# Output projection as seven products of halves, with weight sums made in DRAM and the convolution norm inside attention

## The chip, the cores and the metric

The kernel runs on one core of a Trainium2 chip. The metric is the device time of one execution in microseconds (us); lower is better. The core has five engines with a queue each: TensorE (PE) multiplies matrices into PSUM, VectorE (DVE), ScalarE (ACT) and GpSimd (POOL) work on elements, SyncE (SP) issues DMAs. ScalarE and GpSimd can issue DMAs too. An engine works through its queue in order.

## The reference, cut to what matters

One layer of an encoder: 1024 positions (16 grid rows of 64 columns), 1024 channels, float32.

```python
h = rms_norm(x, norm1_g)
a, gate, q, k, v = split(h @ w_in)                 # 5 x 512 columns
u = a * sigmoid(gate)                              # convolution heads
y = layer_norm(conv31_depthwise(u) + dw_bias, conv_ln_g, conv_ln_b)
conv_out = silu(y)                                 # 1024 x 512
attn_out = neighbourhood_attention(rms_norm(q), rms_norm(k), v, rpb)   # 8 heads of 64
x = x + concat([conv_out, attn_out]) @ w_out       # 1024x1024 @ 1024x1024
h = rms_norm(x, norm2_g)
x = x + (silu(h @ w_gate) * (h @ w_up)) @ w_down   # inner width 2816
```

## The kernel before, in words

Every float32 matmul is made of three fp32r ones: each operand is split into a high part `hi` (a cast, by ScalarE) and a low part `lo` (source minus `hi`, by VectorE or GpSimd; lines 103 to 108), and `mac` (lines 110 to 114) adds hi x hi, hi x lo and lo x hi into one PSUM tile of 128 x 512. So in the profile L104 is a cast, L108 a subtraction, and L112, L113 and L114 are the three matmuls, with the PSUM tile's name before them.

The order of the instructions on each engine is the order of the program, written out by hand. `woven` is a list of small jobs, one of which is run after each `mac` (`weave`), so that other work lies between the matmuls.

The stages, with the profiled times: projections of k, the gated convolution input (gl), q and v until about 241 us, in steps (`step`) of 24 matmuls, with the 31 convolution taps beside them (VectorE's L319, and GpSimd's L345, which adds products `pr` that ScalarE makes); the last sum `u` of both is VectorE's L324. The rows of v go to DRAM (`vd`, L406) and come back as windows (`vw`). Then attention, 32 steps of one pair of heads on 128 queries each: step i multiplies scores s (L615), turns the weights of step i-2 (p, L646), and multiplies them with the values of step i-3 (o, L662). VectorE adds the bias table and takes the row's extreme (L628), ScalarE takes the exponential (L630), GpSimd scales it (L637), VectorE and ScalarE copy one half of the turned weights each (L651). After four steps ScalarE and VectorE write the output as hi and lo (`at`, L669 and L674).

Then the output projection: 8 row tiles, 2 halves of the columns (pj for the first, pk for the second), 8 blocks of 128 inputs. Between the matmuls of the first half the convolution's result is turned (y, L728), normed (L735 to L756), turned back and put through silu (z, L761); its split is `cm`. A finished tile is added to x (L775). With the second half the second norm follows (L857 to L867) and the normed rows xn are turned for h2 (t, L994).

Gate and up are already seven products of halves (m1 to m7) for each of 22 blocks. Their left sides are the quarter A11, A12 (in h2), A22 of the rows and the sums S1 to S4 of quarters, formed of rows (sn, L944) and turned one by one (sq and sp, L963); their right sides are sums of quarters of the weights (ts, L893), split by GpSimd or VectorE. The down product follows, with operands that are summed and split in the same way.

The places that the prediction speaks of are attention's loop and what fills the queues ahead of it; both stand in the functions below.

Of the kernel before, what the change touches and what calls it, by code (L numbers as in the profile page):

```python
# [30 lines left out]
def layout(v):  # L31
# [4 lines left out]
    gu = np.stack([f["w_gate"], f["w_up"]]).reshape(2, KB, P, FB, P).transpose(3, 0, 2, 1, 4)  # L36
    wd = f["w_down"].reshape(FB, P, D)
# [14 lines left out]
        "wo": f["w_out"],  # L52
# [15 lines left out]
def build(ctx, tc, a):  # L68
# [22 lines left out]
    def SM(name, n=8):  # L91
        return T("sm", [P, 8], 16, name)[:, :n]

# [93 lines left out]
    wo, woq = {}, {}  # L187

    def wo_dst(d, k0):
        def dst():  # L190
            if (d, k0 // 4) not in woq:
                woq[d, k0 // 4] = H(f"wo{d}{k0}", F32R)
            q = woq[d, k0 // 4]
            o = k0 % 4 * 1024
            hl = (q[:, o:o + 1024], q[:, o + 1024:o + 2048])
            for j in range(2):
                wo[d, k0 + j] = [w[:, j * 512:(j + 1) * 512] for w in hl]
            return hl
        return dst

    for d in range(2):
        for k0 in (4, 6, 0, 2):
            want(a["wo"][k0 * P:(k0 + 2) * P, d * 512:(d + 1) * 512].rearrange("(k p) m -> p k m", p=P),
                 f"wo{d}{k0}", wo_dst(d, k0), (pool,) * 4 if d == 0 and k0 < 4 else (pool,))
# [204 lines left out]
    pend = []  # L409

    def step(post=None, n_taps=4):
        todo = pend[:]
# [251 lines left out]

    def evac_hi(s_):
        rh, cb = order[s_]
        if rh == 0:
            at[cb] = [G(f"at{cb}{w}", F32R).rearrange("p (c t q) -> p c t q", c=4, t=2) for w in range(2)]
        act.copy(at[cb][0][:, :, rh], os_[s_])  # L669

    def evac_lo(s_, cs=slice(0, 4)):
        rh, cb = order[s_]
        hi, lo = [w[:, cs, rh] for w in at[cb]]
        dve.tensor_tensor(lo, os_[s_][:, cs], hi.bitcast(F32), OP.subtract)  # L674
# [38 lines left out]
    cm, x2, xn = [], {}, {}  # L713

    def lhs(k, t):
        if k < 4:
            return [w[:, k, t * P:(t + 1) * P] for w in cm]
        return [w[:, k - 4, t // 4, :] for w in at[t % 4]]

    def proj(t, d, acc, ks):  # L720
        for k in ks:
            mac(acc, lhs(k, t), wo[d, k], k == 4, k == 3)
            weave()

# [143 lines left out]

# [379 lines left out]
```

## Time and profile before

| | |
|---|---|
| median of 3 runs | 1063.48 us (1063.12 to 1063.6) |
| the profiled execution | 1064.03 us, its span 1062.2 us |
| granted TensorE clock | 0.999 |
| DMA | 144.05 MB in 68244 packets, mean 136 GB/s |

The profile shows one execution; its span runs from the first to the last recorded instruction, and 1.8 us of its time lie outside. "PEld" is the loading of weights into TensorE, which overlaps the matmuls. A row of the view of groups names line, engine, operation, output<-input, shape and count, then the busy time in us and the mean of one in ns, then the engine's idle time before them and what ended it.

### The profile page before, as it was taken

Reading aid. Unit: us, or ns where it says so; the run is one execution under the profiler, and the core shown is the slowest. Engines: PE = TensorE matmul, PEld = TensorE weight load, DVE = VectorE, ACT = ScalarE, POOL = GpSimd, SP = SyncE. Lnnn points to the kernel's source line nnn. Section 1 sums busy time; section 2 is a strip of 40 time slices with the busy share of each in tenths; the row PEclk is TensorE's granted clock in tenths of the full one; section 3 lists DMA queues with packets and bytes.
Section 4 is the critical chain, followed back from the end, with each engine's and each line's share of the span. In section 5 each row is a group of like instructions: output and inputs, shape, how many; then the busy total and the mean of one; then the engine's idle time right before and its main releaser. Section 6 shows DMA issues by size and latency. Waiting matters only on the chain.

```text
span 1062.2 us, 13969 instructions
## 1 busy us (share of the span) xinstructions
PE 1045.4 (98%) x5068; PEld 847.3 (80%) x5068; DVE 699.8 (66%) x1072; ACT 443.7 (42%) x874; POOL 397.3 (37%) x308
## 2 busy tenths in 40 slices
PE   7999999999999999999999999999999999999997
PEld 5788888776667888788888888888888888888886
DVE  6768998966765247666565564564655567858883
ACT  6456346626776334532323223332233344433441
POOL 0126568823542301444554544545454200002310
PEclk9999999999999999999999999999999999999999
DMA  9416681245504412032322222232132597634641
GB/s 333 164 47 225 217 257 36 75 161 154 165 34 161 136 80 99 21 129 77 136 91 104 109 99 95 104 129 100 70 131 78 194 322 276 209 99 132 205 127 43
DMA packets 68244, 144.05 MB, mean 136 GB/s; under 512 B 12496, under 2 KB 21200, under 8 KB 67536
## 3 DMA queue, kind: packets, MB, share of 16 engines
q1 hardware_dynamic: 66336, 139.95, 38.3%
q10 hardware_dynamic: 1840, 3.22, 0.9%
q8 instruction: 40, 0.66, 0.3%
q14 instruction: 28, 0.23, 0.1%
HBM read 103.99 MB, written 44.76 MB: 140 GB/s over the span
## 4 chain that ended last, share of the span: by engine, by line
PE 94%; DMA 2%; DVE 1%; ACT 1%; POOL 1%; issue 0%; SPq 0%; POOLq 0%; ACTq 0%
PE B L112 6%; PE B L114 6%; PE B L113 6%; PE A L112 4%; PE D L112 4%; PE D L114 4%; PE A L114 4%; PE D L113 4%; PE A L113 4%; PE z L113 3%; PE z L112 3%; PE z L114 3%; PE gl L114 3%; PE gl L112 3%; PE gl L113 3%; PE o L662 2%
## 5 line engine op out<-in xcount | busy, mean ns | idle before, releaser
L319 DVE SCALAR_TENSOR_TENSOR cv<-u,par,cv 128x1009 f32<-128x1009 f32 (+14 forms) x85 | 108.5, 1276 | 1.9
L345 POOL TENSOR_TENSOR pa<-pa,pr 128x1022 f32<-128x1022 f32 (+10 forms) x31 | 74.2, 2392 | 35.5 <-ACT pr L344 26.5
L104 ACT CAST op<-sr 128x512 fp32r<-128x512 f32 x77 | 47.7, 619 | 52.1 <-PE B2d L114 26.3
L108 DVE TENSOR_TENSOR op<-sr,op 128x512 fp32r<-128x512 f32 x77 | 57.1, 742 | 16.1 <-ACT op L104 16.0
L1037 DVE TENSOR_TENSOR g<-B,g 128x512 f32<-128x512 f32 x22 | 15.2, 691 | 79.0 <-PE B L114 79.0
L1209 POOL TENSOR_TENSOR ou<-ou,resm 128x512 f32<-128x512 f32 x8 | 12.2, 1530 | 144.0 <-DMA resm<-xd 142.1
L1046 ACT ACTIVATE D<-D 128x512 f32<-128x512 f32 x22 | 12.8, 582 | 113.1 <-DVE D L1045 113.1
L1032 DVE TENSOR_TENSOR u<-B,g 128x512 f32<-128x512 f32 x22 | 15.2, 691 | 62.1 <-PE B L114 62.1
L104 ACT CAST op<-wd 128x512 fp32r<-128x512 f32 x66 | 40.9, 620 | 30.7 <-DVE wd L1124 18.4
L637 POOL TENSOR_SCALAR e<-e,rs 128x288 f32<-128x288 f32 (+1 forms) x64 | 34.1, 545 | 50.2 <-DVE rs L635 42.9
L108 DVE TENSOR_TENSOR op<-wd,op 128x512 fp32r<-128x512 f32 x66 | 50.4, 764 | 1.8
L893 DVE TENSOR_TENSOR ts<-gu,ts 128x512 f32<-128x512 f32 x44 | 51.0, 1159 | 0.8
L1035 ACT ACTIVATE A<-A 128x512 f32<-128x512 f32 x20 | 11.6, 582 | 76.3 <-PE A L114 76.3
L630 ACT ACTIVATE e<-e,mx 128x288 f32<-128x288 f32 (+1 forms) x64 | 36.2, 569 | 2.0 <-DVE mx L628 2.0
L628 DVE CUSTOM_DVE_ANT_0 e<-s,tab 128x288 f32<-128x288 f32 (+1 forms) x64 | 30.1, 505 | 8.1 <-PE s L615 8.0
L344 ACT ACTIVATE pr<-u,par 128x1022 f32<-128x1022 f32 (+10 forms) x31 | 34.2, 1135 | 1.2 <-ACT vs L405 1.2
L893 DVE TENSOR_TENSOR ts<-gu 128x512 f32<-128x512 f32 x22 | 34.1, 1551 | 0.0
L646 PEld LDWEIGHTS p<-ident,e 128*96 128x96 f32 (+1 forms) x192 | 20.1, 133 | 15.2 <-issue 10.5
L944 POOL TENSOR_TENSOR xn<-xn,xn 128x512 f32<-128x512 f32 x4 | 6.9, 1732 | 57.3 <-DVE sn L944 57.3
L646 PE MATMUL p<-ident,e 128*96 128x128 f32 (+1 forms) x192 | 27.6, 280 | 0.7 <-DVE pT L651 0.6
L662 PE MATMUL o<-pT,vw 96*64 96x128 f32 (+1 forms) x384 | 28.0, 281 | 0.0
L615 PE MATMUL s<-kT,qT 64*128 64x288 f32 (+1 forms) x128 | 26.7, 495 | 0.0
(1039 smaller groups left out, 3449.6 us busy)
## 6 DMA issues: line engine op xcount, KB each, us to landing
gu<-in_gu SPq DMA_DIRECT2D x44, 512.0 KB
sr<-sd SPq DMA_DIRECT2D x77, 256.0 KB
sd<-sd SPq DMA_DIRECT2D x22, 512.0 KB
wd<-in_wd SPq DMA_DIRECT2D x44, 256.0 KB
sd<-g SPq DMA_DIRECT2D x33, 256.0 KB
x<-in_x SPq DMA_DIRECT2D x16, 512.0 KB
xd<-x SPq DMA_DIRECT2D x8, 512.0 KB
resm<-xd SPq DMA_DIRECT2D x16, 256.0 KB
```

Source lines behind the costliest of these rows:

```text
L104: act.copy(hi, src)
L108: eng.tensor_tensor(*[w[..., sl] for w in (lo, src, hi.bitcast(F32))], OP.subtract)
L112: pe.matmul(acc, lh, rh, start=start, stop=False, skip_group_check=True)
L113: pe.matmul(acc, lh, rl, start=False, stop=False, skip_group_check=True)
L114: pe.matmul(acc, ll, rh, start=False, stop=stop, skip_group_check=True)
L319: dve.scalar_tensor_tensor(acc[:, o], uc[:, i], dwk[:, c, t:t + 1], acc[:, o], OP.mult, OP.add)
L344: act.activation(pr[:, o], uc[:, i], AF.Copy, scale=dwk[:, c, t:t + 1])
L345: pool.tensor_tensor(pa[:, o], pa[:, o], pr[:, o], OP.add)
L630: act.activation(e[:, hh], e[:, hh], AF.Exp, bias=mx, scale=-1.0, accum_out=rs[:, hh:hh + 1])
L646: pe.transpose(pt[:m, g * P:(g + 1) * P], es[i][:, hh, g * m:(g + 1) * m], ident)
L662: pe.matmul(os_[s_][hh * HD:(hh + 1) * HD, hp], vw[cb, rh + g][:, c:c + HD], pTs[i][:, g, hh], start=g == 0, stop=g == 2)
L893: dve.tensor_tensor(o, l, r, OP.subtract)
```

## The change

Seven things change.

1. `w_out` is laid out as four quarter blocks B11, B12, B21, B22 (rows of attention's or the convolution's channels reversed, so that A11 is attention's output of the lower half of the rows and A12 the convolution's), and a copy of the first four gate/up blocks likewise (`w4`, `g4`).
2. The sums P1 to P4 of these blocks are made in DRAM: ScalarE's queue issues 12 copies (`sum_step` with names that end in c) and GpSimd's 12 accumulating DMAs (names in a), 1 MB or half of it each, at numbered projection steps and, for the last two, in attention's steps 3 and 6.
3. The output projection is seven products n1, n7, n4, n6, n5, n2, n3, of 4 column blocks x 4 input blocks each. n7 is added into the PSUM tiles of n1, and n5 into those of n6, with a read between; `put` adds or subtracts a tile to or from x. Left sides are A11, A12, A22 and the sums Q1 to Q4, which are held as `rf` and `df`, summed by VectorE, and split by ScalarE and GpSimd.
4. In attention's loop every second step from 3 to 17 turns a tile of the convolution and takes its statistics; the square root is made on VectorE by Newton steps in steps 19 to 21, and steps 22 to 29 scale one tile each, in place.
5. The weight parts of the first two products are cast and subtracted in attention, one a step from step 17 on.
6. The normed rows are turned once (`turn`, 64 transposes); A11 and A12 go to h2, and S1 to S4 are summed and split on turned rows.
7. The first four gate/up blocks take their sums from DRAM, their order is m1, m2 of blocks 0 to 3 first, all their splits go to GpSimd, and signs are such that sums are subtracted.

```diff
+    order = [m + h * FB // 2 for m in range(FB // 2) for h in range(2)]
+    gs = gu[order[:4]].reshape(4, 2, P, 2, 512)
+    wq = f["w_out"].reshape(2, 2, 2, P, 2, 512)[::-1].transpose(0, 4, 1, 3, 2, 5)
+    pairs = [(k, d) for k in range(2) for d in range(2)]
+    w4, g4 = [np.stack(w) for w in ([wq[k, d] for k, d in pairs], [gs[:, d, :, k] for k, d in pairs])]
...
+    def sum_step(w, n, i=None):
+        m, op = {"P1": ("B12", "B11"), "P3": ("B12", "B22"), "P2": ("P1", "B22"), "P4": ("P2", "B21")}[n[:2]]
+        rs = slice(0, P) if i is None else slice(64 * i, 64 * i + 64)
+        if n[2] == "c":
+            nc.scalar.dma_start(pw[w, n[:2]][rs], block(w, m)[rs])
+        else:
+            pool.dma_start(pw[w, n[:2]][rs], block(w, op)[rs], accum_op=OP.add, max_dma_last_dim=2048)
...
+    at_step = {
+        5: [("g4", "P1c")], 6: [("g4", "P3c")], 7: halves("P1c"), 8: halves("P3c"), 9: [("g4", "P1a")],
+        11: [("g4", "P3a")], 14: halves("P1a"), 15: halves("P3a"), 24: [("g4", "P2c")], 25: [("w4", "P2c", 0)],
+        26: [("w4", "P2c", 1)], 31: [("w4", "P2a", 0)], 32: [("g4", "P2a")], 33: [("w4", "P2a", 1)],
+        34: [("g4", "P4c")], 35: [("w4", "P4c", 0)], 36: [("w4", "P4c", 1)], 37: [("g4", "P4a")],
+    }
...
+    for n in ("B11", "P3", "P4", "P2", "P1", "B21", "B22"):
+        for j in range(2):
+            want(block("w4", n)[64 * j:64 * j + 64].rearrange("r (h e) -> (r h) e", h=2), f"{n}{j}", wq_dst(n, j))
...
+        n_steps[0] += 1
+        for args in at_step.get(n_steps[0], ()):
+            sum_step(*args)
...
+            for j in range(2):
+                act.copy(rowf[j][:, :, cb], os_[s_][:, 2 * j:2 * j + 2])
+        else:
+            a11[cb] = [w.rearrange("p (c q) -> p c q", c=4) for w in lr(G(f"a11{cb}", F32R))]
+            act.copy(a11[cb][0], os_[s_])
...
+        for j in js:
+            cs = slice(2 * j, 2 * j + 2)
+            hi, lo = [w[:, cs] for w in a11[cb]]
+            dve.tensor_tensor(lo, os_[s_][:, cs], hi.bitcast(F32), OP.subtract)
+            dve.tensor_tensor(diff[j][:, :, cb], os_[s_][:, cs], rowf[j][:, :, cb], OP.subtract)
...
+    LHS = {"n7": "Q3", "n4": "A22", "n6": "Q2", "n5": "Q1", "n2": "A12", "n3": "Q4"}
+    RHS = {"n1": "B11", "n7": "P3", "n4": "P4", "n6": "P2", "n5": "P1", "n2": "B21", "n3": "B22"}
+    CB = (0, 3, 1, 2)
+
+    def proj(p, cb, acc, cs=range(4), start=True):
+        w = wq[RHS[p]]
+        for c in cs:
+            mac(acc, lhs(p, c, cb), [w[:, o + c * 512:o + c * 512 + 512] for o in (0, 2048)],
+                start and c == 0, c == 3)
             weave()
...
+    def q_split(n, f, j, eng):
+        if j == 0:
+            qop[n] = H(n, F32R)
+        split(*[qop[n][:, o + j * 1024:o + j * 1024 + 1024] for o in (0, 2048)],
+              f[j].rearrange("p c b q -> p (c b q)"), (eng,))
...
+    def conv_norm(t):
+        y = conv_T(t)
+        st6 = SM(f"bs{t}", 6)
         dve.bn_stats(st6, y)
...
+        dve.bn_aggr(mvs[:, t], st6)
...
+            xh.extend(lr(G(f"xh{t}")))
+        act.copy(xh[t], y)
...
+        for i in range(3):
+            if i == 2:
+                yield
+            dve.tensor_tensor(q, g, g, OP.mult)
+            dve.scalar_tensor_tensor(q, q, 0.25 ** i, w, OP.mult, OP.mult)
+            dve.scalar_tensor_tensor(g, q, -3.0, g, OP.add, OP.mult)
...
+    def conv_scale(t, eng):
+        eng.tensor_scalar(xh[t], xh[t], mvs[:, t, 0:1], rc[:, t:t + 1], op0=OP.subtract, op1=OP.mult)
...
+    def conv_diff(h, c, y4):
+        tiles = lambda w: w.rearrange("p (b i j) -> p i b j", b=4, j=16)
+        d, r = [tiles(w[c // 2][:, c % 2].rearrange("p b q -> p (b q)")) for w in (diff, rowf)]
+        dve.tensor_tensor(d, y4, d, OP.subtract if h else OP.add)
+        if h == 0:
...
+    def put(t, d, acc, op=OP.add, eng=dve):
+        w = x2[t][:, d * 512:(d + 1) * 512]
+        eng.tensor_tensor(w, w, acc, op)
...
+    def read(p, cb):
+        acc = pb[cb]
+        if p == "n1":
+            put(4 + cb, 0, acc)
+            put(4 + cb, 1, acc, OP.subtract)
+        elif p == "n7":
+            put(cb, 1, acc, OP.subtract)
+            put(cb, 0, acc)
+        elif p in ("n4", "n6"):
+            put(cb, 0, acc, OP.add if p == "n4" else OP.subtract)
+        elif p == "n5":
+            put(cb, 1, acc)
+            put(4 + cb, 1, acc)
+            norm2(cb)
+        elif p == "n2":
+            put(4 + cb, 0, acc)
+        else:
+            put(4 + cb, 1, acc)
+            norm2(4 + cb)
+
+    while pos[0] < pos[1] + 3:
+        issue()
...
-        if i in (6, 12):
-            load_window(i // 6)
-        if i in (14, 22):
+        if i in (6, 18):
+            load_window(1 + i // 18)
+        if i in (17, 21, 25, 29):
             take_parts(jobs)
...
+        if i % 2 and i < 19:
+            conv_norm(i // 2 - 1)
+        if i == 19:
+            root = rsqrt(rc, mvs[:, :, 1], "rc")
+        if 19 <= i < 22:
+            next(root)
+        if 22 <= i < 30:
+            conv_scale(i - 22, dve)
+        if i == 33:
+            act.activation(warm, eps, AF.Silu)
+            conv_silu(0, 0)
...
+    SRC = {"m6": "P2", "m5": "P1", "m7": "P3", "m3": "B22", "m4": "P4"}
+    firsts = [(i, None) for i in range(4)] + [(p, pr) for pr in range(2) for p in SRC]
+    queue = firsts + [(i, j) for i in range(4, FB) for j in range(2)]
...
-    products = [(i, p) for p in ("m1", "m2", "m6", "m5", "m7", "m4", "m3") for i in range(2)]
-    products += [(i, p) for i in range(2, FB) for p in ORDER]
+    products = [(i, p) for k in (0, 2) for p in ("m1", "m2") for i in (k, k + 1)]
+    products += [(i, p) for k in (0, 2) for p in SRC for i in (k, k + 1)]
+    products += [(i, p) for i in range(4, FB) for p in ORDER]
...
+    def turn(t, j):
+        if not h2:
+            h2.extend(H(f"h2{w}", F32R).rearrange("p (k s) -> p k s", s=512) for w in range(2))
+        pt = (tp, mm)[j](f"t2{t}{j}")
+        for i in range(4):
+            kb = 4 * j + i
+            pe.transpose(pt[:, i * P:(i + 1) * P], xn[t][:, kb * P:(kb + 1) * P], ident)
+        if j == 0:
+            xT[t] = G(f"xT{t}")
+        w = lr(xT[t])[j]
+        if t < 4:
+            hi, lo = [q[:, 4 * j:4 * j + 4, t * P:(t + 1) * P] for q in h2]
+            p3 = pt.rearrange("p (k s) -> p k s", s=P)
+            act.copy(hi, p3)
+            act.copy(w, pt)
+            rest.append(lambda: dve.tensor_tensor(lo, p3, hi.bitcast(F32), OP.subtract))
         else:
...
-    def t2_one(kb):
-        pt = tp(f"t20{kb}")
-        for i in range(4):
-            pe.transpose(pt[:, i * P:(i + 1) * P], xn[i][:, kb * P:(kb + 1) * P], ident)
-        split(h2[0][:, kb, :512], h2[1][:, kb, :512], pt, (dve,))
...
+    for cb in CB:
+        load_x2(4 + cb)
+    weaves(12, s0=lambda: (weigh(31), evac_hi(7), evac_lo(7)), s1=QS("Q3", diff, 0, pool), s2=lambda: tails.pop()(), s3=lambda: read("n1", 0),
+           s4=QS("Q3", diff, 1, pool), s6=C(0, 1), s10=take)
+    group("n1", CB[1:])
+    for cb in CB:
+        load_x2(cb)
+    weaves(16, s1=C(0, 2), s5=take, s9=C(0, 3), s13=QS("Q2", diff, 0, pool))
+    group("n7")
+    weaves(16, s0=C(1, 0), s2=QS("Q2", diff, 1, pool), s4=take, s6=C(1, 1), s9=take, s12=QS("Q1", rowf, 0, pool))
+    group("n4")
+    weaves(16, s0=C(1, 2), s2=take, s5=C(1, 3), s7=QS("Q1", rowf, 1, pool), s10=take, s13=QS("Q4", diff, 0, pool))
+    group("n6")
+    weaves(16, s1=take, s3=QS("Q4", diff, 1, pool), s6=take, s9=N(0), s13=N(3))
+    group("n5")
+    while pos[0] < len(chunks):
+        issue()
...
+    plan = {
+        0: dict(s0=U(7, 0), s1=[U(7, 1), N(5)], s2=SP("S2", 0), s3=SS(3, 1, 2)),
+        1: dict(s0=U(5, 0), s1=[U(5, 1), N(6)], s2=SP("S2", 3), s3=SS(1, 1, 2)),
+        2: dict(s0=U(6, 0), s1=[U(6, 1), lambda: act.activation(warm, eps, AF.Silu)], s2=SP("S2", 1), s3=SS(2, 1, 2)),
+        3: dict(s0=SP("S2", 2), s2=SP("S1", 0), s3=SP("S1", 3)),
...
-            dve.tensor_tensor(l, acc, l, OP.add)
+            dve.tensor_tensor(l, acc, l, OP.subtract)
```

Counted over the program, TensorE goes from 4116 to 4068 matmuls of 512 columns and from 344 to 296 transposes of 128 columns; the others stay.

ScalarE's queue at the end of the projections, before (pr is a product for GpSimd's convolution taps, vs a tile of v):

```order
L344 ACTIVATE pr_1918<-u_1310,par 128x1013
L405 ACTIVATE vs_1952<-z_1886,r_104 128x512
L406 DMA vd<-vs_1952 128x512
L344 ACTIVATE pr_1959<-u_1310,par 128x1012
L405 ACTIVATE vs_1991<-z_1927,r_104 128x512
L406 DMA vd<-vs_1991 128x512
L405 ACTIVATE vs_2023<-z_1966,r_104 128x512
```

and now:

```order
L371 ACTIVATE pr_1908<-u_1330,par 128x1014
L432 ACTIVATE vs_1937<-z_1868,r_112 128x512
L433 DMA vd<-vs_1937 128x512
L371 ACTIVATE pr_1944<-u_1330,par 128x1013
L208 DMA g4P_72<-g4P_70 16x16384
L432 ACTIVATE vs_1979<-z_1911,r_112 128x512
L433 DMA vd<-vs_1979 128x512
L371 ACTIVATE pr_1986<-u_1330,par 128x1012
L208 DMA w4P_68<-w4P_66 16x8192
L432 ACTIVATE vs_2019<-z_1953,r_112 128x512
L433 DMA vd<-vs_2019 128x512
L208 DMA w4P_68<-w4P_66 16x8192
```

Three copies (L208, 2 MB in all) now stand among the last products pr, the stores of v and what follows them, the first exponentials.

GpSimd's queue at the same place, before (pa is the sum of taps, e the attention weights):

```order
L345 TENSOR_TENSOR pa_1620<-pa_1620,pr_1838 128x1016
L345 TENSOR_TENSOR pa_1620<-pa_1620,pr_1841 128x1015
L345 TENSOR_TENSOR pa_1620<-pa_1620,pr_1883 128x1014
L345 TENSOR_TENSOR pa_1620<-pa_1620,pr_1918 128x1013
L345 TENSOR_TENSOR pa_1620<-pa_1620,pr_1959 128x1012
L637 TENSOR_SCALAR e_2066<-e_2066,rs_2067 128x288 x2
L637 TENSOR_SCALAR e_2109<-e_2109,rs_2110 128x288 x2
```

and now:

```order
L210 DMA w4P_66<-in_w 256x512
L372 TENSOR_TENSOR pa_1643<-pa_1643,pr_1862 128x1016
L372 TENSOR_TENSOR pa_1643<-pa_1643,pr_1865 128x1015
L210 DMA g4P_70<-in_g 512x512
L372 TENSOR_TENSOR pa_1643<-pa_1643,pr_1908 128x1014
L210 DMA w4P_66<-in_w 256x512
L372 TENSOR_TENSOR pa_1643<-pa_1643,pr_1944 128x1013
L372 TENSOR_TENSOR pa_1643<-pa_1643,pr_1986 128x1012
L210 DMA g4P_72<-in_g 512x512
L668 TENSOR_SCALAR e_2096<-e_2096,rs_2097 128x288 x2
L668 TENSOR_SCALAR e_2139<-e_2139,rs_2140 128x288 x2
L210 DMA w4P_68<-in_w 256x512
```

Five accumulating DMAs (L210) stand among the last sums of taps and the first scalings of e; the one ahead of L668 adds into what ScalarE's first copy writes.

VectorE's queue in one of attention's later steps, before:

```order
L628 ISA e_3007,mx_3009<-s_2991,tab_2356 128x384
L628 ISA mx_3009 128x1
L628 ISA e_3007,mx_3012<-s_2993,tab_2356 128x384
L628 ISA mx_3012 128x1
L651 COPY pT_3005<-p_2998 128x3x128
L674 TENSOR_TENSOR at_2824<-o_2851,at_2823 128x2x128
L635 RECIPROCAL rs_3008<-rs_3008 128x2
```

and now, where a scaling of the convolution (xh) and two residues fall together:

```order
L659 ISA e_3155,mx_3157<-s_3139,tab_2418 128x384
L659 ISA mx_3157 128x1
L659 ISA e_3155,mx_3160<-s_3141,tab_2418 128x384
L659 ISA mx_3160 128x1
L682 COPY pT_3153<-p_3146 128x3x128
L825 TENSOR_SCALAR xh_2678<-xh_2678,par 128x512
L718 TENSOR_TENSOR a_3098<-o_2986,a_3098 128x256
L719 TENSOR_TENSOR df_2536<-o_2986,rf_2342 128x2x128
L666 RECIPROCAL rs_3156<-rs_3156 128x2
```

The scaling and a second residue are added between the copy of the turned weights and the reciprocal.

391 lines of the change are left out of this document (187 added, 204 removed).

## The prediction

> **What bounds the kernel now.** I read the page first: the busy time of each engine, the granted clock and the chain of work that ended last.
>
> ```profile
> span 1062.2 us, 13969 instructions
> PE 1045.4 (98%) x5068; PEld 847.3 (80%) x5068; DVE 699.8 (66%) x1072; ACT 443.7 (42%) x874; POOL 397.3 (37%) x308
> PEclk9999999999999999999999999999999999999999
> PE 94%; DMA 2%; DVE 1%; ACT 1%; POOL 1%; issue 0%; SPq 0%; POOLq 0%; ACTq 0%
> ```
>
> TensorE is busy for 98% of the span, carries 94% of the chain, and its clock is full in every slice. The view of its waits then tells how much of the rest is a wait on another engine (line, engine waited for, total us, times, longest):
>
> ```profile
> PE z L112 <- ACT wk0h L104: 6.9, 1, 6.9
> PE z L113 <- POOL w23l L108: 0.7, 1, 0.7
> PE p L646 <- DVE pT L651: 0.6, 1, 0.6
> PE t L994 <- DVE xn L867: 0.6, 1, 0.6
> ```
>
> Apart from the first weights there is no wait of 1 us. So in the part that the change touches, work taken from TensorE is worth its own duration, as long as the other engines keep up. The prices come from two views: the table of windows (length, then busy us and instruction count of PE, PEld, DVE, ACT and POOL, then clock, DMA share and GB/s), and pieces of the chain (start, us, what).
>
> ```profile
> 100.00:150.00 50.00, 50.00 (x223) 41.40 (x222) 45.80 (x44) 19.43 (x21) 32.83 (x17) 1.00 0.79 245
> 260.00:311.00 51.00, 51.00 (x467) 33.12 (x468) 38.83 (x139) 39.62 (x120) 28.93 (x52) 1.00 0.35 112
> 290.00:311.00 21.00, 21.00 (x190) 13.51 (x188) 16.00 (x56) 16.55 (x50) 12.73 (x23) 1.00 0.20 64
> 600.00:800.00 200.00, 200.00 (x884) 165.62 (x883) 109.49 (x133) 59.26 (x108) 100.64 (x75) 1.00 0.29 106
> ```
>
> ```profile
> 296.86 0.85 PE s L615 x4
> 297.71 0.81 PE p L646 x6
> 298.51 0.81 PE o L662 x12
> 320.76 0.44 PE y L728 x4
> 395.95 0.44 PE t L994 x4
> 425.54 0.44 PE sq L963 x4
> 428.49 0.89 PE sp L963 x8
> ```
>
> From 600 to 800 us TensorE does nothing but 512-column matmuls: 200 / 884 = 0.2262 us each. Four 128-column transposes cost it 0.44 us, eight 0.89. One attention step with a 384-column window is 0.85 + 0.81 + 0.81 = 2.47 us by its pieces; from one s piece to the next I use 2.44.
>
> **The change, term by term.** The sum is made against the profiled execution, 1064.03 us, which is 0.55 us above the median of the runs.
>
> *Products of halves.* Before, the output projection is 8 row tiles x 2 column halves x 8 k blocks x 3 matmuls = 384; after it, 7 products x 4 column blocks x 4 k blocks x 3 = 336. That is 48 x 0.2262 = 10.9 us less on the chain.
>
> *Rows turned once.* Before, the second norm's rows are turned in 8 groups for h2 and 20 for S1 to S4 and A22, four transposes each; after it, in 16. That is 12 x 0.44 = 5.3 us less. The 32 conv transposes (y) only move into attention, and the 32 of z stay beside the projection: nothing.
>
> Together 16.1 us less, to 1047.9, if nobody makes TensorE wait. The following terms ask that.
>
> *Conv norm in attention.* VectorE's rows by shape, and one of ScalarE's (count, then busy us and mean ns):
>
> ```profile
> L735 DVE BATCH_NORM_STATS2 bs<-y 128x6 f32<-128x512 f32 x8 | 5.6, 695 | 2.4 <-PE y L728 2.4
> L755 DVE SCALAR_TENSOR_TENSOR bb<-bm,br 128x1 f32<-128x1 f32 x6 | 1.8, 304 | 0.4 <-DVE br L747 0.2
> L752 DVE TENSOR_SCALAR xh<-y,bm,br 128x512 f32<-128x512 f32 x2 | 1.6, 810 | 0.1
> L736 DVE BATCH_NORM_AGGREGATE bm<-bs 128x2 f32<-128x6 f32 x8 | 1.5, 182 | 0.3
> L674 DVE TENSOR_TENSOR at<-o,at 128x256 fp32r<-128x256 f32 x12 | 4.9, 412 | 0.0
> L775 DVE TENSOR_TENSOR x<-pk,x 128x512 f32<-128x512 f32 x8 | 5.5, 687 | 6.0 <-PE pk L114 6.0
> L104 ACT CAST wo<-wo04r 128x256 fp32r<-128x256 f32 x4 | 1.6, 391 | 0.0
> ```
>
> In steps 3 to 17 every second step gets statistics (0.695 + 0.182 us on VectorE) but also 0.44 us of transposes. VectorE needs 38.83 / 51 of the time there, 1.86 us of 2.44; 2.74 of 2.88 in such a step is still under. The tight place is steps 19 to 29: 11 x 2.44 = 26.8 us of TensorE, in which VectorE now has 11 x 1.86 = 20.4. Added are 14 instructions of the square root by Newton steps on 128x8, with no row of their own, between 0.18 (the aggregate's) and 0.30 us (the 128x1 row): 2.5 to 4.2. Two more of the 0.41 us residues fall there: 0.8. Eight scalings of 512 columns run from SBUF in place; the nearest rows are 0.41 (half the columns, two inputs) and 0.81 (the same operation out of PSUM): 3.3 to 6.5. So VectorE needs 27.0 to 31.9 us of 26.8: a loss of 0 to 5. I take 2, under the middle, because a row's exponentials are read two steps later, which lets about a step's slack absorb a peak. ScalarE has 16.55 of 21 there, 1.92 a step, and gains one 128x256 cast a step (0.39): 2.3 of 2.44, no loss by itself.
>
> The Trainium skill, page "VectorE: DVE Perf Modes", section "Why PSUM operands drop a tier", says that fp32 tensor_scalar reads at double rate from SBUF and not from PSUM; by its tier table I estimate 0.42 us. With that, the lower end of the loss would be the likely one and the sum 2 us less. No row of before shows that form. The page "GPSIMD Engine Reference", section "Specifications", speaks against it: such two-port instructions contend with GpSimd, which is at work here in each step.
>
> *Hand-over from the first product to the second.* n7 accumulates in n1's four banks, each of which VectorE must first add into two tiles. On VectorE's queue stand 4 residues of attention's last output, then conv's difference, which waits for GpSimd's half of Q3, and behind it the adds.
>
> ```profile
> L104 ACT CAST w23h<-w23r x1: 1032/1032/1032, 191.6 to 191.6; 128x1024 fp32r<-128x1024 f32 x1
> L108 POOL TENSOR_TENSOR w23l<-w23r,w23h x1: 2399/2399/2399, 195.6 to 195.6; 128x1024 fp32r<-128x1024 f32 x1
> ```
>
> A half is 128x1024: cast 1.03, subtraction 2.40. Counted from the second block of n1: 0.7 for three matmuls, 0.8 for the last o, 0.6 for ScalarE's copy of it (between its 0.39 and 1.03), two residues 0.8, cast and subtraction 3.4, then two conv sums and two adds at 0.69: 9.1. TensorE asks for the bank after 36 matmuls (8.1), that o (0.8) and one turning (0.4): 9.3. The margin is about zero; each us of lag from attention goes against it. Between nothing and 2 us lost, I take 0.7. The later products leave VectorE 1 to 2 adds per 2.7 us and need nothing that tight.
>
> *Sums of weight blocks in DRAM.* ScalarE's queue issues 12 copies, GpSimd's 12 accumulating DMAs, some 8 MB each; before has no accumulating one. Their issues, and SP's 12 more DMA issues, lie beside TensorE's matmuls. What matters is who stands behind. Timeline rows of GpSimd, VectorE, ScalarE and TensorE (start, us), and the longest load on the chain:
>
> ```profile
> 208.97 7.29 POOL L345 TENSOR_TENSOR pa<-pa,pr 128x1014 f32<-128x1014 f32 x3 [0.52 <-ACT pr L344]
> 231.38 0.99 POOL L637 TENSOR_SCALAR e<-e,rs 128x288 f32<-128x288 f32 x2 [15.11 <-DVE rs L635]
> 228.15 1.22 DVE L324 TENSOR_TENSOR u<-cv,pa 128x1024 f32<-128x1024 f32 x1
> 209.43 0.33 ACTq L406 DMA_DIRECT2D vd<-vs  x1
> 212.44 1.14 ACT L344 ACTIVATE pr<-u,par 128x1012 f32<-128x1012 f32 x1 [0.40 <-ACT vs L405]
> 240.98 0.86 PE L646 MATMUL p<-ident,e 128*96 128x128 f32 x6
> 13.06 7.97 DMA ag10r<-in_ag
> ```
>
> GpSimd issues g4's P2 sum at about 209; ScalarE's copy to P4 waits for it, with the last conv product and the stores of v behind; GpSimd's sum into P4 waits for the copy, with the first scaling of e behind (231.4, read by TensorE at 241.0). GpSimd has 22 us, and 8.6 more before TensorE notices: 31. The sum moves about 3.1 MB and the copy 2.1. At the 245 GB/s of the busiest window that is 13 + 9 = 22 us; two 512 KB loads like ag10r, one for each, doubled for 1 MB, give 32. So 0 to 1 us, and I take 0. ScalarE's wait ends at 222 at the 13 us, and the conv product of 212.4 starts 10 us late; its sum, which GpSimd ended at 216.3, is read by VectorE at 228.15, 12 us later. That cover is thin: without it u and with it the first scores are late, 1:1.
>
> *The rest.* Minus signs cost nothing. For the first four gate/up blocks the DRAM sums replace VectorE's, and GpSimd makes one split of some 1.4 us per product of 12 matmuls (2.7), which is free. VectorE and ScalarE now split turned rows: in the first eight products VectorE has 12 residues, 10 sums and one 1024-column scaling, 24 x 0.69 = 17 us, or, beside GpSimd at the price of
>
> ```profile
> L893 DVE TENSOR_TENSOR ts<-gu,ts 128x512 f32<-128x512 f32 x44 | 51.0, 1159 | 0.8
> L108 POOL TENSOR_TENSOR t2m<-gu,t2m 128x512 fp32r<-128x512 f32 x3 | 4.4, 1451 | 5.3 <-ACT t2m L104 5.3
> ```
>
> 22 x 1.16 + 1.4 = 27 us, against 24.3 of TensorE (eight products, six turnings). Products of S2 begin only with the ninth, those of S1 with the eleventh, so I take nothing.
>
> The sum: 1064.0 - 10.9 - 5.3 + 2.0 + 0.7 = 1050.5; less 0.55 is 1050.0 for a median.
>
> **Rivals.**
>
> *VectorE becomes the bound in attention.* For: the 31.9 of 26.8 at the upper prices, and a peak at steps 27 and 28, where two residues and a scaling fall together. Against: its idle time now, 24% there. With 5 us there and 2 at the hand-over: 1047.9 + 7 - 0.5 = 1054.4; up to 1059 if 5 us more go in steps 3 to 18, where it needs 2.74 of 2.88 us in every second step.
>
> *The DMA chain stops GpSimd before the first e scaling: slower than before.* One place, one price: TensorE pays 1:1 for each us by which sum plus copy exceed 31. The forecast gain is gone, and 2.1 us more, at 31 + 13.5 + 2.1 = 47 us. At 64 GB/s, the lowest rate of a window above, the sum alone takes 49 us, with 9 for the copy 58: 27 late, so 1050 + 27 = 1077. Against: that window is slow because little was asked for. The Trainium skill, page "DMA: Bandwidth & Descriptors", section "Issuing engines are not separate DMA queues", says that transfers of all issuers run on the same 16 engines, and "Anatomy of one DMA" gives a fit of 2 us plus the bytes at 436 GB/s, which I estimate as 4.4 us each; by it this rival is out, but no run shows an accumulating transfer.
>
> *Gain not delivered.* If weight loads or tables come late because 16 MB more are moved beside a window with a DMA share of 0.79, TensorE waits in the projections; 10 us late gives 1060, and near 1062 it is no change. Against: outside that window the share is 0.2 to 0.4.
>
> **How the numbers follow.** The measurement can tell about 0.2%, 2.1 us, from no change. The likeliest case, both savings with 0 to 5 us lost, has 0.62 (1046.5 to 1052.5); VectorE as the bound 0.20 (1052.5 to 1059); late loads 0.08, half of it within 0.2%; the DMA chain 0.10, nearly all slower. Faster is 0.62 + 0.20 + 0.04 = 0.86, same 0.04, slower 0.10. For 8 in 10 the range runs from 1046 (no loss at all gives 1047.4, and the short waits p and t may go) to 1059.
>
> **What would show it.** Right: 48 fewer 512-column matmuls and 48 fewer transposes, PE busy near 1029 us, and a PE wait list without a new entry above 1 us except on VectorE between steps 19 and 29 and at the start of n7. Wrong: a wait of p on GpSimd's e near 231 to 245, an idle stretch of TensorE behind ScalarE's copies, or VectorE at 100% in 290 to 320 with p or s waiting in each step.

## The result: slower by 1.2%

The changed kernel takes 1075.66 us (median of 4 runs, 1072.17 to 1079.1) against 1063.53 before: a ratio of 1.0115, interval 1.0082 to 1.0148. That is 12 us slower where 13.5 us faster was forecast. The profiled execution took 1075.09 us, span 1073.3. Lines of its page:

```profile
span 1073.3 us, 13909 instructions
PE 1037.3 (97%) x4972; PEld 838.5 (78%) x4972; DVE 723.2 (67%) x1097; ACT 463.1 (43%) x911; POOL 456.5 (43%) x342
...
PEclk9999978999999999999999999999999999999999
...
q0 software_dynamic: 4288, 8.39, 4.7%
...
PE 71%; DMA 10%; POOL 5%; issue 5%; SPq 3%; DVE 3%; ACT 3%; ACTq 0%; POOLq 0%; DVEq 0%
...
g4P<-in_g POOLq DMA_DIRECT2D x4, 1024.0 KB, 11.6
w4P<-in_w POOLq DMA_DIRECT2D x8, 512.0 KB, 9.1
```

The saving is there: 96 matmuls and transposes fewer. But TensorE's part of the chain of work that ended last fell from 94% to 71%, that of transfers rose from 2% to 10%, and the granted clock dips in the sixth and seventh slice (about 134 to 188 us). Queue q0, new, is GpSimd's 12 accumulating DMAs; the last two rows are their issues with the median time from issue to landing. TensorE's waits:

```profile
PE z L122 <- ACT wk0h L114: 7.4, 1, 7.4
PE z L122 <- ACT w02h L114: 4.1, 1, 4.1
PE o L693 <- DMA vw<-vd: 3.3, 1, 3.3
PE z L123 <- POOL pa L367: 2.2, 1, 2.2
PE z L123 <- POOL w01l L118: 1.9, 1, 1.9
PE z L123 <- POOL w02l L118: 1.6, 1, 1.6
PE p L677 <- DVE rcq L818: 1.5, 2, 1.2
PE t L1054 <- DVE xn L950: 1.2, 1, 1.2
PE B L124 <- POOL t0m L118: 1.1, 1, 1.1
PE B L122 <- DVE u L1172: 0.8, 1, 0.8
```

Of these the list of before has the first and, with 0.6, the one on xn. Four belong to the splitting of q's weights (w01r to w03r are the rows as loaded, h and l their high and low parts; the row that names pa is the wait for w03l), long before any code that the output projection touches. To see how much is lost where, take the row of the attention outputs in the view by tile: count, then shortest, median and longest ns, then first and last start. Before, and after:

```profile
L662 PE MATMUL o<-pT,vw x384: 272/273/324, 243.9 to 319.6; 96*64 96x128 f32 x96, 128*64 128x128 f32 x96
```

```profile
L693 PE MATMUL o<-pT,vw x384: 272/273/476, 261.6 to 347.7; 96*64 96x128 f32 x96, 128*64 128x128 f32 x96
```

| us | to the first o | first to last o | last o to the end | span |
|---|---|---|---|---|
| before | 243.9 | 75.7 | 742.6 | 1062.2 |
| after | 261.6 | 86.1 | 725.6 | 1073.3 |
| difference | +17.7 | +10.4 | -17.0 | +11.1 |

**The first stretch.** The table of windows from 60 to 100 and from 130 to 170 us (columns as in the prediction), before and after:

```profile
60.00:100.00 40.00, 40.00 (x186) 33.09 (x185) 30.14 (x35) 27.75 (x86) 22.09 (x10) 1.00 0.41 130
...
130.00:170.00 40.00, 40.00 (x182) 33.14 (x181) 35.40 (x38) 19.29 (x25) 28.73 (x14) 1.00 0.64 186
```

```profile
60.00:100.00 40.00, 40.00 (x185) 33.09 (x185) 30.42 (x36) 27.78 (x86) 24.20 (x12) 1.00 0.84 207
...
130.00:170.00 40.00, 29.54 (x103) 22.14 (x102) 27.95 (x24) 12.30 (x13) 23.08 (x11) 0.75 0.80 258
```

From 60 to 100 us nothing is lost, and the DMA engines are busy at 0.84 instead of 0.41. The bill comes later: from 130 to 170 TensorE issues 103 matmuls instead of 182, at a mean clock of 0.75. TensorE's timeline there, after:

```profile
146.98 0.39 PE L124 MATMUL z<-w00h,hT 128*128 128x512 f32 x1
147.99 0.50 PE L122 MATMUL z<-w01h,hT 128*128 128x512 f32 x1 [0.62 <-ACT w01h L114]
150.42 0.80 PE L123 MATMUL z<-w01l,hT 128*128 128x512 f32 x1 [1.93 <-POOL w01l L118]
...
157.02 0.79 PE L122 MATMUL z<-w02h,hT 128*128 128x512 f32 x1 [4.10 <-ACT w02h L114]
...
164.55 0.79 PE L123 MATMUL z<-w03l,hT 128*128 128x512 f32 x1 [2.17 <-POOL pa L367]
...
169.84 0.63 PE L123 MATMUL z<-w01l,hT 128*128 128x512 f32 x1
170.27 0.49 PE L124 MATMUL z<-w01h,hT 128*128 128x512 f32 x1
170.59 0.40 PE L122 MATMUL z<-w01h,hT 128*128 128x512 f32 x1
```

From 147.21, where the last undisturbed matmul's 0.226 us end, to 170.59 there are 23.4 us with 27 matmuls, which at full clock are 6.1. Five waits are 10.5 us (0.62, 1.93, 4.10, 1.65, 2.17). Of the other 6.8, up to 5.4 go to the clock: matmuls start 0.43 us apart (169.84 to 170.27) instead of 0.23, at a granted clock of 0.50 from 150 to 170 us, until 6 us after the last wait. The rest lies at the ends and restarts around the waits. So 10.5 us of waiting cost 17.3.

ScalarE, which makes the high parts, waits for the transfer itself. Its cast of w01, before and after:

```profile
129.54 1.05 ACT L104 CAST w01h<-w01r 128x1024 fp32r<-128x1024 f32 x1 [1.06 <-DMA w01r<-in_qkv]
```

```profile
146.89 1.05 ACT L114 CAST w01h<-w01r 128x1024 fp32r<-128x1024 f32 x1 [14.47 <-DMA w01r<-in_qkv]
```

GpSimd isn't held up ahead of this: its half of ag13 starts at 112.39 before and at 112.38 after. Before, it had the low parts of w01, w02 and w03 ready 11, 7 and 4 us ahead of their first matmuls. That was all the slack there was.

Why q's weights are late is told by SP's queue, which loads them in order between the bias tables. The same issues, before and after (start, us):

```profile
125.19 0.53 SPq L141 DMA_DIRECT2D w01r<-in_qkv  x1
...
133.45 0.53 SPq L141 DMA_DIRECT2D w02r<-in_qkv  x1
```

```profile
143.00 0.53 SPq L151 DMA_DIRECT2D w01r<-in_qkv  x1
...
151.25 0.53 SPq L151 DMA_DIRECT2D w02r<-in_qkv  x1
```

Both start the tables at the same time (66.2 and 66.5); w01 and w02 are issued 17.8 us later in the changed kernel, and the lag grows on the way: 8.1 us at ag13 (89.19 and 97.29), 16.2 at ag03 (101.39 and 117.59). SP's own longest waits for transfers between 63 and 160 us (us in total, times, longest), before and after:

```profile
SPq L481 <- DMA t<-neg: 0.6, 1, 0.6
```

```profile
SPq L507 <- DMA t<-in_rpb: 6.0, 3, 3.4
SPq L512 <- DMA tf<-neg: 3.6, 4, 2.4
SPq L512 <- DMA t<-in_rpb: 2.2, 1, 2.2
```

Before, SP waits 0.6 us for transfers in that stretch: it issues without a gap. After, it waits for its small table transfers to land, 11.8 us in these three rows; shorter waits and issues that take longer make up the rest of the 17.8. In the trace SP's issues use eight semaphores in turn, and each waits for the transfer that used its semaphore before. So when transfers land later, the whole queue slows.

**The second stretch.** ScalarE's timeline at the end of the projections:

```profile
235.48 0.69 ACT L432 ACTIVATE vs<-z,r 128x512 f32<-128x512 f32 x1 [7.28 <-DMA g4P<-in_g]
...
244.66 0.69 ACT L432 ACTIVATE vs<-z,r 128x512 f32<-128x512 f32 x1 [6.36 <-DMA g4P<-g4P]
```

The first wait is that of the copy to g4's P4 for the sum into g4's P2. The second, at a copy to w4's P4, ends with the landing of the copy to g4's P4, which used the same semaphore. The scaling of v and its stores stand behind both: TensorE then waits 3.3 us for v's reload (vw).

### The profile page after: what moved, and what is told of

It is laid out like the page before. It is cut to its first block, busy times and chain, and to the rows that moved or that the text cites. A ratio compares the mean times of both kernels' runs of the same rounds, so it can differ in the third digit from the quotient of the medians.

```text
span 1073.3 us, 13909 instructions
## 1 busy us (share of the span) xinstructions
PE 1037.3 (97%) x4972; PEld 838.5 (78%) x4972; DVE 723.2 (67%) x1097; ACT 463.1 (43%) x911; POOL 456.5 (43%) x342
## 3 DMA queue, kind: packets, MB, share of 16 engines
q0 software_dynamic: 4288, 8.39, 4.7%
q10 hardware_dynamic: 2224, 11.61, 3.0%
## 4 chain that ended last, share of the span: by engine, by line
PE 71%; DMA 10%; POOL 5%; issue 5%; SPq 3%; DVE 3%; ACT 3%; ACTq 0%; POOLq 0%; DVEq 0%
PE B L122 5%; PE B L123 5%; PE B L124 5%; PE D L122 4%; PE D L123 4%; PE D L124 4%; PE A L122 3%; PE A L123 3%; PE A L124 3%; PE z L123 2%; PE z L122 2%; PE z L124 2%; DMA t<-in_rpb 2%; DMA vd<-vs 2%; PE o L693 2%
## 5 line engine op out<-in xcount | busy, mean ns | idle before, releaser
L114 ACT CAST op<-wd 128x512 fp32r<-128x512 f32 x66 | 40.8, 619 | 29.8 <-DVE wd L1267 17.3
L668 POOL TENSOR_SCALAR e<-e,rs 128x288 f32<-128x288 f32 (+1 forms) x64 | 34.6, 553 | 39.5 <-DVE rs L666 23.4
L976 DVE TENSOR_TENSOR ts<-ts,gu 128x512 f32<-128x512 f32 x36 | 43.3, 1202 | 0.6
L1178 ACT ACTIVATE A<-A 128x512 f32<-128x512 f32 x18 | 10.5, 582 | 68.6 <-PE A L124 68.6
L863 DVE TENSOR_TENSOR x<-x,n 128x512 f32<-128x512 f32 x40 | 26.1, 680 | 18.0 <-PE n L124 11.0
L976 DVE TENSOR_TENSOR ts<-gu 128x512 f32<-128x512 f32 x18 | 30.0, 1665 | 0.0
L693 PEld LDWEIGHTS o<-pT,vw 96*64 96x64 f32 (+1 forms) x384 | 20.7, 138 | 9.4 <-issue 5.8
## 6 DMA issues: line engine op xcount, KB each, us to landing
g4P<-in_g POOLq DMA_DIRECT2D x4, 1024.0 KB, 11.6
```

The source lines that it names most:

```text
L114: act.copy(hi, src)
L668: pool.tensor_scalar(es[i][:, hh], es[i][:, hh], rs[:, hh:hh + 1], 1.0, op0=OP.mult, op1=OP.mult)
L693: pe.matmul(os_[s_][hh * HD:(hh + 1) * HD, hp], vw[cb, rh + g][:, c:c + HD], pTs[i][:, g, hh], start=g == 0, stop=g == 2)
L976: dve.tensor_tensor(lr(tsum[i, 1])[n - 3] if o is None else o, l, r, OP.add)
```

## The experiments

All are medians against runs of the kernel before on the same chip (1063.3 to 1063.6).

### Is it the sums, and are they enough alone?

e1_no_sums, the change with all 24 DMAs taken out and plain blocks in the sums' places:

```diff
-        return a[w][BLK[n]] if n in BLK else pw[w, n]
+        return a[w][BLK.get(n, int(n[1]) - 1)]
     def sum_step(w, n, i=None):
+        return
```

> The changed kernel without its 12 copies and 12 accumulating DMAs: the products read unsummed weight blocks, so the output isn't the reference's; everything else is as in the change. Theory A (the sums' traffic slows SP's queue of small bias-table transfers, so that q's weights land late and TensorE waits and loses its clock) and theory B (ScalarE and GpSimd stand still behind waits for the sums) both say 1049 to 1055 us, the forecast's 1050 with its small stalls. Theory C (the loss is in attention, the hand-over and the turned rows) says 1068 or more.

Measured: 1056.65 us (1052.19 to 1058.87), ratio 0.9931 (0.9906 to 0.9957). Without the DMAs the change is faster than before, but by less than the sum said, and just outside the 1049 to 1055 expected. A wait of 4.9 us at the hand-over between the first products is in its profile, where VectorE's adds wait for the loads of x's rows.

e2_before_sums, the kernel before with the same 24 DMAs and nobody who reads them:

```diff
+        for args in at_step.get(n_steps[0], ()):
+            sum_step(*args)
```

> The kernel before, with the same 12 copies and 12 accumulating DMAs at the same steps, whose results nobody reads. Theory A: 17 to 27 us over before, 1080 to 1090, with a wait of z for w01 to w03 of 10 us or more. Theory B: 5 to 12 us over before, 1069 to 1075, and no wait for w01 to w03. Theory C: within 3 us of before.

Measured: 1085.48 us (1084.82 to 1087.81), ratio 1.0211 (1.0196 to 1.0227): +22 us, with the waits of the changed kernel (w02h 3.9, vw 3.5, pa 2.2, w01l 1.9). The sums cost 22 us in the kernel before too, which doesn't use them. In the changed kernel leaving out all 24 DMAs gave 19 us (1075.7 to 1056.7).

### Which part of them?

e4_copies_only leaves out GpSimd's accumulating DMAs, e3_small_copies cuts the copies into 2 KB rows:

```diff
-            pool.dma_start(pw[w, n[:2]][rs], block(w, op)[rs], accum_op=OP.add, max_dma_last_dim=2048)
+            pass
```

```diff
-            nc.scalar.dma_start(pw[w, n[:2]][rs], block(w, m)[rs])
+            nc.scalar.dma_start(pw[w, n[:2]][rs], block(w, m)[rs], max_dma_last_dim=2048)
```

> The changed kernel with the 12 copies and without the 12 accumulating DMAs, so the output isn't the reference's. If the copies (16 rows of 64 KB) make SP's queue late: 1066 to 1074, with the waits for w01 to w03 still there. If the accumulating DMAs do: 1050 to 1058, without those waits. If bytes alone count, half of the delay of SP's queue goes: 1058 to 1066.

> The changed kernel with its copies written as rows of 2 KB in place of 64 KB, the same bytes. If large pieces ahead of the small table transfers are what delays them: 1052 to 1065 and shorter waits for w01 to w03. If the bytes are: 1072 to 1080, unchanged.

Measured: e4 1052.63 us (1051.23 to 1054.46), ratio 0.9904 (0.9887 to 0.9920); e3 1075.76 (1073.75 to 1080.65), ratio 1.0123 (1.0096 to 1.0149), which is the changed kernel's time. The copies cost nothing that shows where they lie, and neither does the size of their pieces. But the first six are issued at 53 to 60 us, ahead of the tables (67.7), so e4 alone doesn't tell whether adding or place makes the difference. In e4's profile all waits on w01 to w03 are gone and attention begins as before:

```profile
L693 PE MATMUL o<-pT,vw x384: 272/273/324, 243.7 to 324.7; 96*64 96x128 f32 x96, 128*64 128x128 f32 x96
```

e6_plain_pool answers that: it keeps GpSimd's 12 DMAs at their places and takes only the accumulation out:

```diff
-            pool.dma_start(pw[w, n[:2]][rs], block(w, op)[rs], accum_op=OP.add, max_dma_last_dim=2048)
+            pool.dma_start(pw[w, n[:2]][rs], block(w, op)[rs], max_dma_last_dim=2048)
```

> The changed kernel with GpSimd's 12 accumulating DMAs as plain copies of the same blocks, rows, places and waits, so the sums are missing and the output isn't the reference's. If it is the adding that occupies the DMA engines: 1051 to 1057, as with the copies of ScalarE's queue alone, and no wait for w01 to w03. If it is GpSimd's way of issuing, whatever is moved: 1070 to 1078, as in the change. If it is traffic in the stage of the tables, of which a plain copy makes about half: 1057 to 1066.

Measured: 1062.27 us (1058.14 to 1065.86, 10 runs), ratio 0.9985 (0.9972 to 0.9998). From its page, and the row of o:

```profile
q0 software_dynamic: 2240, 8.39, 2.2%
...
g4P<-in_g POOLq DMA_DIRECT2D x4, 1024.0 KB, 7.4
w4P<-in_w POOLq DMA_DIRECT2D x8, 512.0 KB, 6.7
```

```profile
L693 PE MATMUL o<-pT,vw x384: 272/273/325, 251.8 to 332.7; 96*64 96x128 f32 x96, 128*64 128x128 f32 x96
```

Plain transfers of the same bytes take 2.2% of the 16 engines' span, 23 us, and accumulating ones 4.7%, 50 us; half of the bytes of each are issued beside the tables (69 to 104 us). SP issues w01 at 125.53 in e4, 134.33 here and 143.00 in the changed kernel: 9 and 17.5 us late, nearly in proportion to that time. Attention begins 8 and 18 us late. With 9 us of lag TensorE waits for w02 and w03 (0.7, 1.9 and 3.4 us) and not for w01, as the slack of 11, 7 and 4 us says. So traffic of GpSimd's queue slows the small transfers on SP's queue, even without adding, and with accumulation the lag is twice as long. That engine time is what they share is the likeliest reading, but not shown by itself: the packets double as well (2240 and 4288), and packet times can overlap, as DMA shares above 1 in short windows show (1.05 from 90 to 100 us). The number of packets alone can't be it on ScalarE's queue, where e3 had 6128 in place of 2224 for 3.2% in place of 3.0%.

### Does another queue for q's weights help?

e11_w0_on_act issues w00 to w03 on ScalarE's queue:

```diff
-            nc.sync.dma_start(d, src)
+            (nc.scalar if name[:2] == "w0" else nc.sync).dma_start(d, src)
```

> The changed kernel, sums as they were, with q's four weight loads (w00 to w03) issued by ScalarE's queue in place of SP's. Theory: the sums only delay SP's queue, and TensorE waits because these loads stand in that queue behind some 80 table transfers. Then TensorE's wait in 145 to 170 us goes, the tables stay late: 1056 to 1066. If the loads themselves are slowed by the traffic: 1070 to 1078.

Measured: 1069.12 us (1067.27 to 1070.98), ratio 1.0046 (1.0032 to 1.0061): 6.5 us back of the 23 by which the change lies above e4, and between the two ranges expected. The waits that named w01 to w03 are gone, but the gate's last weights (ag03, issued at 118.32) still stand behind the tables, and TensorE waits 1.8 us for their half and 3.4 for VectorE's u; vw's 3.8 stays.

### Can the sums lie elsewhere?

e7_late_sums moves them all behind the tables, from the last projection steps into attention and the output projection, and loads P3 one step later:

```diff
-        5: [("g4", "P1c")], 6: [("g4", "P3c")], 7: halves("P1c"), 8: halves("P3c"), 9: [("g4", "P1a")],
+    at_step = {34: [("w4", "P1c")], 35: [("w4", "P3c")]}
+    in_attn = {
+        2: [("w4", "P1a")], 3: [("w4", "P3a")], 7: [("w4", "P2c")], 11: [("w4", "P2a")], 15: [("w4", "P4c")],
...
```

> The changed kernel with all sums moved behind the bias tables: w_out's from the last projection steps into attention's step 19, gate/up's from attention's step 20 into the product n5; the load of P3 goes one step later. Same results. If the sums cost only where they delay SP's queue of table transfers and the first windows of v: 1049 to 1055, faster than before. If they cost wherever they run: 1066 or more.

Measured: 1073.53 us (1073.11 to 1074.1), ratio 1.0092 (1.0075 to 1.0109): a miss for 1049 to 1055. Attention begins on time (first o at 243.6) but takes 96.5 us instead of e4's 81.0. TensorE's waits:

```profile
PE p L679 <- DVE pT L684: 9.2, 3, 7.8
...
PE p L679 <- POOL e L670: 3.2, 7, 0.9
```

e8_fitted_sums puts w4's P1 and P3 into the first steps, whole, ahead of the tables, the rest where the DMA share before was low, with g4's last three in attention steps 9, 12 and 16. e9_fitted_x_early is e8 with half of x's rows loaded earlier, to take away the wait for x that e1 showed:

```diff
+        1: [("w4", "P1c")], 2: [("w4", "P3c")], 7: [("w4", "P1a"), ("w4", "P3a")],
+        24: [("g4", "P1c")], 25: [("g4", "P3c")], 26: [("w4", "P2c")], 27: [("g4", "P1a")], 28: [("g4", "P3a")],
+        29: [("w4", "P2a")], 32: [("w4", "P4c")], 34: [("w4", "P4a")], 36: [("g4", "P2c")],
+    in_attn = {9: [("g4", "P2a")], 12: [("g4", "P4c")], 16: [("g4", "P4a")]}
```

> The changed kernel with the sums moved to the stretches in which the DMA engines have room and no short transfer is waited for: w_out's P1 and P3 ahead of the bias tables, its P2 and P4 and gate/up's P1 and P3 behind them (160 to 220 us), gate/up's P2 and P4 in attention's steps 9 to 16. Same results. If what counts is which transfers the sums lie beside: 1050 to 1058. If accumulating costs wherever it runs, as the late version suggests: 1066 or more.

> The one before, and x's rows for n7 are loaded ahead of the weight P21 in SP's queue. Theory: the load of x's rows, which now waits behind a weight buffer that GpSimd frees, is what VectorE's adds and so n7 wait for, 0 to 5 us from run to run. Then 1 to 5 us below the one before and a smaller spread. If the adds are late by VectorE's own work, as the forecast had it: no difference.

Measured: e8 1066.24 us (1060.68 to 1071.97, 12 runs), ratio 1.0023 (1.0001 to 1.0044); e9 1064.36 (1061.7 to 1068.81, 12 runs), ratio 1.0011 (0.9999 to 1.0024). Both miss what was expected of them: e8 lies at the edge of its range for "costs wherever it runs", and e9 gains 1.9 us on it, within the spread. Both lose nothing before attention (first o at 243.7 in e8) and then 7 to 8 us at one place. ScalarE's timeline in e9:

```profile
273.14 0.48 ACTq L208 DMA_DIRECT2D g4P<-g4P  x1
273.72 0.47 ACT L682 COPY pT<-p 96x384 f32<-96x384 f32 x1 [7.57 <-DMA g4P<-in_g]
```

The copy to P4 stands three steps (7.3 us) behind the sum into P2, which takes 16.3 us to land; ScalarE waits for it with its share of pT behind, and TensorE waits 7.0 us for pT. In e7 ScalarE stands at a copy too, for 8.71 us, but there the wait ends with a load of v's windows (vw) on SP's queue, which used the same semaphore. Either way the queue's order gives a copy's wait to the pT behind it. This place doesn't explain all of e8: its profile is that of its fastest run, 1060.7, and others took up to 1072.

Against e9, e12_spaced and e14_apart move only those three: to steps 7, 15 and 23, and to step 18 of attention and the products n4 and n5 of the output projection. The edit of e14:

```diff
-    in_attn = {9: [("g4", "P2a")], 12: [("g4", "P4c")], 16: [("g4", "P4a")]}
+    in_attn = {18: [("g4", "P2a")]}
-    weaves(16, s0=C(1, 0), s2=QS("Q2", diff, 1, pool), s4=take, s6=C(1, 1), s9=take, s12=QS("Q1", rowf, 0, pool))
+    weaves(16, s0=C(1, 0), s2=QS("Q2", diff, 1, pool), s3=X("g4", "P4c"), s4=take, s6=C(1, 1), s9=take, s12=QS("Q1", rowf, 0, pool))
-    weaves(16, s1=take, s3=QS("Q4", diff, 1, pool), s6=take, s9=N(0), s13=N(3))
+    weaves(16, s1=take, s3=QS("Q4", diff, 1, pool), s5=X("g4", "P4a"), s6=take, s9=N(0), s13=N(3))
```

> The fitted version with x's rows early, and gate/up's last three transfers moved apart in attention: P2's sum at step 7, P4's copy at 15, P4's sum at 23 (before 9, 12, 16). Theory: the fitted version lost its time where ScalarE's queue waited 7.6 us for a sum that took 16.3 us to land and had been given 3 steps, 7.3 us; 8 steps are 19.5 us. Then the wait of p for pT of 7 us goes: 1050 to 1056, faster than before. If traffic in attention costs by itself: 1060 to 1066, as the fitted one.

> The spaced version with gate/up's last transfers away from the loads of v's windows and the last bias table: P2's sum at attention's step 18, P4's copy in the product n4, P4's sum in n5. Theory: the spaced version still lost about 6 us where a table of 1.5 MB landed 19 us after its issue beside P2's sum; then 1052 to 1057 and no wait of p of more than 1.5 us. If a sum costs the same wherever it lies: 1058 to 1064.

Measured: e12 1058.93 us (1056.09 to 1065.26, 12 runs), ratio 0.9969 (0.9951 to 0.9988); the 7 us are gone, but it misses the 1050 to 1056 expected. Its profile, of a run of 1064.6 us, has two waits of 3.6 us. One is for x's rows. The other, put down to rcq, stands behind VectorE, which waits 3.2 us for a bias table. That table took 19.0 us to land, but it was also issued 5.5 us later than in e14 (271.95 and 266.50), at the end of the sum into P2 (252.4 to 272.6) and not beside it. So in attention, too, a sum can make SP's loads late; which load it slowed isn't followed here. e14: 1053.54 us (1052.52 to 1056.27, 6 runs), ratio 0.9909 (0.9893 to 0.9924). The kernel computes all that the change computes and beats both kernels, before by 0.9% and the change by 22 us. Its page, TensorE's waits and the row of o:

```profile
PE 1028.2 (98%) x4972; PEld 833.9 (79%) x4972; DVE 718.9 (68%) x1097; ACT 463.4 (44%) x911; POOL 450.6 (43%) x338
...
g4P<-in_g POOLq DMA_DIRECT2D x4, 1024.0 KB, 14.3
```

```profile
PE z L122 <- ACT wk0h L114: 6.2, 1, 6.2
PE gl L124 <- POOL ag10l L118: 1.4, 1, 1.4
PE p L680 <- DVE rcq L821: 1.3, 1, 1.3
```

```profile
L696 PE MATMUL o<-pT,vw x384: 272/273/324, 244.3 to 325.9; 96*64 96x128 f32 x96, 128*64 128x128 f32 x96
```

A sum still takes 14.3 us, and TensorE waits for none; ScalarE waits 1.7 us and SP up to 14.0 us for one, without a wait of TensorE behind them.

### What is left of the spread?

e13_no_sums_x_early is e1 with x's rows earlier:

```diff
+    for cb in CB:
+        load_x2(cb)
...
-    for cb in CB:
-        load_x2(cb)
```

> The kernel without sums (output not the reference's), with x's rows for n7 loaded ahead of the weight P21 in SP's queue. Theory: the spread of the one without sums (1052 to 1059) and its wait of n on x of 4.9 us come from the load of x's rows behind that weight. Then 1050 to 1053 with a spread under 3 us and no such wait. If the adds are late by VectorE's own work: 1052 to 1059 again.

Measured: 1054.37 us (1050.92 to 1056.87, 6 runs), ratio 0.9912 (0.9894 to 0.9929), against e1's 1056.65. The wait for x falls from 4.9 to 2.2 us in the profiles, but the runs still spread by 6 us, so both expectations, no such wait and a spread under 3 us, are missed. Why e1, with less traffic than e4, is not faster than it, and where the spread comes from, stays open.

## Why the prediction was wrong, step by step

**The step that failed** is "Sums of weight blocks in DRAM": that the DMAs' issues "lie beside TensorE's matmuls", so "I take 0". I asked there only who waits for a sum. The loss comes first from who shares the DMA engines with it: SP's queue of small table transfers, with q's weight loads in order behind. e4 and e6 show it from both sides. In the changed kernel the term that was put at nothing is 17.7 us before attention (table above) and 86.1 - 81.0 = 5.1 in it, 22.8 together; e2 measured 22 for it alone.

**The rival that named it**, "Gain not delivered", had the right mechanism ("weight loads or tables come late") and the right doubt about the window with share 0.79, but a chance of 0.08 and 10 us. Its argument against, that elsewhere the share is 0.2 to 0.4, looked at the mean share of the engines. It asked neither that SP's queue issues without a gap (0.6 us of waits), so that slower landings add to its lag, nor how much slack q's weights had (4 to 11 us). The queue lost 8 us before 100 us already, where the share had been 0.41. And 10.5 us of waits cost 17.3, mostly since the clock fell; no step reckoned with the clock. The chance of 0.10 for a slower kernel rested on the other rival, below, and not on this one. The Trainium skill, page "DMA: Bandwidth & Descriptors", section "Issuing engines are not separate DMA queues", was used in the prediction against a rival only; what it says, that transfers of all issuers interleave on the same 16 engines, agrees with e6, where plain transfers of GpSimd's queue made SP's loads 9 us late, and it spoke against this change. The estimate of 4.4 us for each from the same page's "Anatomy of one DMA" is out by far: 11.6 us median accumulating, 7.4 plain.

**The rival on the slower side**, that the DMA chain stops GpSimd ahead of the first e, held only in part: GpSimd waited 4.28 us for the copy to g4's P4, and its first scaling came at 251.66 instead of 231.38, 20.3 us late of which 17.7 are the late start of attention. The sum took 9.3 us and the copy 9.1, less together than the 22 to 32 reckoned. The chain cost some 5 us through ScalarE's queue, which the prediction named, with v's stores behind the copy. But its 12 us of cover were reckoned for u and not for v's reload; the two waits there are 13.6 us, and TensorE waited 3.3 for vw.

**The other terms held, one of them in part by luck.** Products and turnings: 16.2 us forecast. In e4 TensorE is busy 1028.4 us, 17.0 less than before; 1029 was forecast. From the last o to the end the changed kernel saves 17.0; 16.2 and the 3.5 us of conv transposes that moved into attention (8 x 0.44) would be 19.7, less 0.7 at the hand-over (n's wait for x, as forecast) and 2.5 in new short waits (xn 1.2 instead of 0.6, t0m 1.1, u 0.8), which the prediction took as nothing: 16.5. The agreement at the hand-over is luck. The prediction counted VectorE's work there, but the adds wait for the loads of x's rows, which it left out, and TensorE's wait was 4.9 us in e1, 3.6 in e12, 2.2 in e13 and none in e14. Attention: 81.0 - 75.7 - 3.5 = 1.8 us lost in e4, 2.0 forecast; 1.5 of it is the wait for the square root (rcq). VectorE's forms, in after:

```profile
L825 DVE TENSOR_SCALAR xh<-xh,par 128x512 f32<-128x512 f32 x8 | 5.4, 678 | 0.0
L820 DVE SCALAR_TENSOR_TENSOR rcg<-rcq,rcg 128x8 f32<-128x8 f32 x3 | 1.0, 330 | 0.1
```

The scaling out of SBUF takes 0.68 us, between the bounds of 0.41 and 0.81; the 0.42 us estimated from the Trainium skill's page "VectorE: DVE Perf Modes" doesn't show beside a busy GpSimd. The small root instructions come to 3.3 us, of 2.5 to 4.2. With the sums out of the way the forecast of 1050.5 us for a profiled execution stands beside 1051.43 in e4, 1053.21 in e14 and 1053.41 in e13, but 1057.62 in e1, with its wait for x.

## What to carry to other kernels

Ask of added DMA traffic not only who waits for it, but which queue of small, ordered transfers shares the engines at that time: read that queue's own waits before, and if it has none because it issues without a gap, any slowing adds up in the loads in order behind it until their slack is used up. An engine whose queue issues a DMA that waits for another gives that wait to all behind it, so dependent DMAs go apart by more than the landing time of the first. Lay such traffic where nobody's load is under way: the same sums cost 22 us at one place and nothing that shows at another (1053.5 us in e14, against 1052.6 in e4 without accumulating and 1054.4 in e13 without any).

## What was not expected of the hardware

- An accumulating DMA between DRAM tensors took twice the engine time of a plain one of the same bytes (50 us of 16 engines against 23 for 8.39 MB, in 4288 packets against 2240), and 11.6 us median from issue to landing against 7.4 for 1 MB.
- After waits of 0.62 and 1.93 us with one matmul between, the granted clock was halved already, and it came back only 6 us after the last wait. The Trainium skill, page "TensorE: Matmul & The Clock Gate", section "What's actually happening", states that the clock halves after an idle window of about 3.4 us; here two shorter waits, 2.55 us together, were enough, so the measurement decides. How little idle time would do, no run here shows.
